# Moving an attention's softmax scaling from VectorE to GpSimd in a one-core hybrid layer

## The chip, the core and the metric

The kernel runs on one core of a Trainium2 chip. A core has a matrix engine (TensorE, PE in the profile; its weight loads are shown as PEld), a vector engine (VectorE, DVE), a scalar engine (ScalarE, ACT), GpSimd (POOL), and a queue engine that issues transfers (SyncE, SP). Each engine takes its instructions in order; engines wait for each other by semaphores. SBUF is the working memory, PSUM the memory that TensorE writes. The metric is the time of one execution in microseconds (us).

## What is computed

One layer of a diffusion backbone over 1024 latent tokens and 256 context tokens, width 1024: a modulated norm, one input projection, a gated delta-rule scan (4 heads of 128, forward and backward), a neighbourhood attention (8 heads of 64), an output projection, and a feed-forward part. The change is in the attention. Each latent query has one softmax over a window of keys and all context keys:

```python
s_win = jnp.einsum("bnqhd,binchd->bhnqic", q_r, k_r).astype(jnp.float32) + bias.astype(jnp.float32)
s_win = jnp.where(col_valid[:, :, None, :], s_win, -jnp.inf)
s_ctx = jnp.einsum("bnqhd,bkhd->bhnqk", q_r, k_ctx).astype(jnp.float32)
s = jnp.concatenate([s_win.reshape(B, H, N_COL_BLK, QB_W, n_win), s_ctx], axis=-1)
p = jax.nn.softmax(s, axis=-1).astype(v.dtype)
...
o = (jnp.einsum("bhnqic,binchd->bnqhd", p_win, v_r)
     + jnp.einsum("bhnqk,bkhd->bnqhd", p[..., n_win:], v_ctx))
```

## The kernel before

The attention is cut into 32 pairs: 4 couples of heads, 2 halves of the grid's rows, 4 blocks of columns. A pair holds two heads u = 0 and 1, each with 128 queries in the partitions and 640 keys (384 of the window, 256 of the context) along a row. So there are 64 heads' tiles in all, and of each small operation below 64.

For one head, `pair` does this. TensorE writes the scores to a PSUM slot `sc` (L100, from `qs`, `kh`, `kl`). VectorE adds the bias tile `bt` to them, writes the sum into `bt` and takes the row maximum into the small tile `mx` (L342, a custom instruction with a second record that reads the maximum out). The maximum is negated (L343), ScalarE takes the exponential of `bt` in place with the row sum (L344), the sum's reciprocal is taken (L345), and `bt` is multiplied by it (L346). In the next step TensorE transposes `bt` in five pieces into another `sc` slot (L104), ScalarE copies them to `pt` (L355), TensorE multiplies with the values (L100, `pt` with `vc` and `vw`), and the result goes to `na` on ScalarE and VectorE (L367, L368).

Buffers tie pairs together. `sc` has three slots, so the transposes of a pair's second head wait for L342 of the next pair's first head, and the next scores for L342 of its second. `bt` has five tiles: before a tile is filled, `biases` clears its context part on GpSimd (L305) and loads the table from `rpb` through SP (L306); both wait until the transposes of five tiles earlier have read it.

The attention runs beside the scan. `fill` is the attention's generator, and the scan's loop takes 0.72 of a step of it after each step of its own. The scan's work on VectorE is L1197, L1208, L1220, L1227 and L1237. In the second half of its ten rounds each chunk is also closed by `finish`: squares (L1252), a reciprocal root on four columns in a chain of tiny operations (L198 to L203), a product (L1258), a transpose of `oacc` (L104) and L1266 to L1268. The last round also starts the output projection: `two_blocks` loads `ew`, and GpSimd takes its low parts (L1292).

What is written in this order is then put in another by a scheduler: it keeps the dependencies and lists each engine's instructions by when it reckons them ready. The order of the engines' instructions is thus a result of the build, and a changed line can move its neighbours.

Of the kernel before, what the change touches and what calls it, by code (L numbers as in the profile page):

```python
# [14 lines left out]
OP = mybir.AluOpType  # L15
# [74 lines left out]
def hybrid(ctx, tc, a, dbg):  # L90
    nc = tc.nc
    act, dve, pool, sp = nc.scalar, nc.vector, nc.gpsimd, nc.sync
# [195 lines left out]
    def attention(nw):  # L288

        def load(hd):  # L290
            qs = nw.tile([128, L], F16, name="qs", tag="qs", bufs=4)
            kh = nw.tile([128, T], F16, name="kh", tag="kh", bufs=4)
            kl = nw.tile([128, T], F16, name="kl", tag="kl", bufs=4)
            sp.dma_start(qs, nq_d[hd].rearrange("i d t -> (i d) t"))
            for i in range(2):
                sp.dma_start(kh[i * 64:i * 64 + 64], nk_d[0, hd])
                sp.dma_start(kl[i * 64:i * 64 + 64], nk_d[1, hd])
            return qs, kh, kl

        def biases(hp, half, cb):  # L300

            out = []
            for u, w0 in enumerate(WIN):
                bt = nw.tile([128, 640], F32, name="bt", tag="bt", bufs=5)
                pool.memset(bt[:, CTX[w0]], 0.0)  # L305
                sp.dma_start(bt[:, w0:w0 + 384], a["rpb"][2 * hp + u, half, CASE[cb]])  # L306
                out.append(bt)
            return out

        def values(hp, half, cb):  # L310
            vw = nw.tile([128, 3, 128], F32, name="vw", tag="vw", bufs=3)
            sp.dma_start(vw, vw_d[:, cb, half:half + 3, hp * 128:hp * 128 + 128])
            return vw

        def context(hp):
            vc = nw.tile([128, 2, 128], F32, name="vc", tag="vc")
            sp.dma_start(vc, nv_d[0:CT, hp * 128:hp * 128 + 128].rearrange("(c p) d -> p c d", p=128))
            return vc

        def slot():  # L320
            return psum[-1].tile([128, 1024], F32, name="sc", tag="sc", bufs=3)

        def pair(heads, bts, vw, vc, half, cb, out):

            r0 = 4 * half
            mx = nw.tile([128, 2, 4], F32, name="mx", tag="mx", bufs=3)
            for u, (head, w0, bt) in enumerate(zip(heads, WIN, bts)):
                qs, kh, kl = head
                sc = slot()[:, AT[u]:AT[u] + 640]
                q = qs[:, (half * 4 + cb) * 128:(half * 4 + cb + 1) * 128]  # L330
                kv = [kx[:, CT:].rearrange("p (r c) -> p r c", c=64)[:, r0:r0 + 12, BLKS[cb]:BLKS[cb] + 32]
                      for kx in (kh, kl)]
                parts = [(CTX[w0].start, CTX[w0].stop, (kh[:, 0:CT], kl[:, 0:CT]))]
                if w0:
                    parts += [(256, 512, [x[:, 0:8] for x in kv]), (512, 640, [x[:, 8:12] for x in kv])]
                else:
                    parts += [(0, 384, kv)]
                for n0, n1, ks in parts:
                    for i in range(2):
                        pe.matmul(sc[:, n0:n1], q, ks[i], start=i == 0, stop=i == 1)  # L340
                m = mx[:, u]
                dve.tensor_tensor_reduce(bt, sc, bt, 1.0, -3.0e38, OP.add, OP.max, m[:, 0:1])  # L342
                dve.tensor_scalar(m[:, 1:2], m[:, 0:1], -1.0, None, op0=OP.mult)  # L343
                act.activation(bt, bt, AF.Exp, bias=m[:, 1:2], accum_out=m[:, 2:3])  # L344
                dve.reciprocal(m[:, 3:4], m[:, 2:3])  # L345
                dve.tensor_scalar(bt, bt, m[:, 3:4], None, op0=OP.mult)  # L346
            yield 1
            pts = []
            for u, bt in enumerate(bts):
                held = slot()  # L350
                sc = held[:, AT[u]:AT[u] + 640]
                for j in range(5):
                    pe.transpose(sc[:, j * 128:(j + 1) * 128], bt[:, j * 128:(j + 1) * 128], ident)
                pt = nw.tile([128, 640], F32, name="pt", tag="pt", bufs=3)
                act.copy(pt, sc)  # L355
                pts.append(pt)
            yield 1
            o = held[:, AT[1] + 640:AT[1] + 768]
            for j in range(5):
                for u, (w0, pt) in enumerate(zip(WIN, pts)):  # L360
                    vals = [vc[:, i] for i in range(2)] + [vw[:, i] for i in range(3)]
                    vv = (vals[j] if w0 else vals[(j + 2) % 5])[:, u * ND:u * ND + ND]
                    pe.matmul(o[u * ND:u * ND + ND], vv, pt[:, j * 128:(j + 1) * 128], start=j == 0, stop=j == 4)
            hi, lo = (out[:, i, half * 512:half * 512 + 512].rearrange("p (r b c) -> p r b c", r=8, b=4)[:, :, cb]
                      for i in range(2))
            o = o.rearrange("p (r c) -> p r c", r=8)
            act.copy(hi, o)  # L367
            dve.tensor_tensor(lo, o, hi.bitcast(F32), OP.subtract)  # L368
            yield 1

        order = [(hp, half, cb) for hp in range(NAH // 2) for half in range(2) for cb in range(4)]
        heads = {0: [load(0), load(1)]}
        vcs = {0: context(0)}
        bt, vw = biases(*order[0]), values(*order[0])
        yield 1
        old = None
        for n, (hp, half, cb) in enumerate(order):
            if half == 1 and cb in (0, 2) and hp + 1 < NAH // 2:
                heads.setdefault(hp + 1, []).append(load(2 * hp + 2 + cb // 2))
                if cb == 0:  # L380
                    vcs[hp + 1] = context(hp + 1)
            cur = pair(heads[hp], bt, vw, vcs[hp], half, cb, na[hp])
            next(cur)
            if old:
                next(old)
            if n + 1 < len(order):
                bt, vw = biases(*order[n + 1]), values(*order[n + 1])
            yield 1
            if old:
                next(old)  # L390
            old = cur
            yield 1
        next(old)
        yield 1
        next(old)
# [967 lines left out]
    class Stream:  # L1363
# [67 lines left out]
        def next(self, n=2):  # L1431

            while len(self.got) < n:
                self.make()
            out = [self.got.pop(0) for _ in range(n)]
            return out
# [400 lines left out]
```

## Time and profile before

| | |
|---|---|
| median of 3 runs | 1521.46 us (1518.48 to 1524.15) |
| the profiled execution | 1521.66 us, span 1519.9 us |
| attention beside the scan | about 553 to 780 us of the span |
| POOL busy in 553 to 680 and 680 to 780 us | 10.99 and 10.56 us |
| granted TensorE clock, mean | 0.99 of full speed |

A row of the stretches shows, for each engine, its busy time. A row of the groups shows line, engine, operation, tiles written and read, shapes and count, then busy us and mean ns of one, then the engine's idle time before it and who ended it. A row of the waits says which engine at which line waited for whom: total us, times, longest. A row of the timeline has start, duration, engine, line and operation, with the idle time before it in brackets. Some matmul records can be missing, and a matmul's record is longer than the time to the next one, since matmuls are pipelined.

### The profile page before, as it was taken

To read this page: it belongs to the slowest core of one execution; us is meant where nothing else is said; L and a number is where in the kernel's file an instruction comes from. 1 tells how busy PE (TensorE), PEld (TensorE's weight loads), DVE (VectorE), ACT (ScalarE), POOL (GpSimd) and SP (SyncE) were. 2 spreads that over 40 slices of the span, in tenths; PEclk is the share of its full clock that TensorE was granted. 3 is DMA by queue.
4 is the path that set the end of the run, shared out by engine and by line. 5 is a ranking of instruction groups with operands and counts; after the bars stand their busy time and mean duration, and the time that the engine had idled before them with its cause. 6 is when DMAs were issued, how large, how long until landed. Compare 5 with 4: busy or idle time off the path is not lost.

```text
span 1519.9 us, 23452 instructions
## 1 busy us (share of the span) xinstructions
PE 1455.5 (96%) x8365; PEld 1208.0 (79%) x8365; DVE 1010.1 (66%) x1908; ACT 703.1 (46%) x1379; POOL 183.3 (12%) x251
## 2 busy tenths in 40 slices
PE   6999998899999998999898999999999999999998
PEld 3789787678877777888787888788888888888887
DVE  4787579455677436779977398766665556699652
ACT  5443461674366545656733284333333334354441
POOL 0154500343134300000100000000000000000000
PEclk9999999999999999999999999999999999999999
DMA  9377133565477798999529415333333335798752
GB/s 368 113 229 238 54 94 122 198 170 176 135 214 251 223 289 239 284 269 274 178 76 322 139 35 183 122 105 103 104 102 101 105 104 172 259 366 284 235 153 83
DMA packets 209829, 276.28 MB, mean 182 GB/s; under 512 B 15968, under 2 KB 116912, under 8 KB 208688
## 3 DMA queue, kind: packets, MB, share of 16 engines
q1 hardware_dynamic: 208992, 274.41, 56.3%
q8 instruction: 66, 1.08, 0.3%
q14 instruction: 51, 0.42, 0.1%
q10 hardware_dynamic: 720, 0.37, 0.1%
HBM read 209.93 MB, written 68.98 MB: 184 GB/s over the span
## 4 chain that ended last, share of the span: by engine, by line
PE 45%; DVE 4%; DMA 2%; ACT 1%; issue 1%; SPq 0%; DVEq 0%; ACTq 0%
PE ps L100 42%; PE sc L100 2%; DMA wad<-wa 1%; PE sc L104 1%; DVE x L1591 1%; DVE ulo L1422 1%; DVE acc L254 0%; DMA wraw<-w_out 0%; DVE x L1567 0%; DVE bt L342 0%; DVE lT L1562 0%; DVE x L1470 0%; ACT x L1571 0%; DVE lB L1575 0%; DMA f_d<-g 0%
## 5 line engine op out<-in xcount | busy, mean ns | idle before, releaser
L100 PE MATMUL ps<-hT,uhi 128*128 128x512 f32 x496 | 146.9, 390 | 1.5 <-DVE e L1712 1.4
L100 PE MATMUL ps<-lT,uhi 128*128 128x512 f32 x496 | 146.5, 390 | 0.0
L100 PE MATMUL ps<-hT,ulo 128*128 128x512 f32 x496 | 146.3, 390 | 0.0
L100 PE MATMUL blk<-hh,whi 128*128 128x512 f32 (+1 forms) x456 | 138.8, 397 | 1.9 <-ACT hh L724 1.5
L100 PE MATMUL blk<-hh,wlo 128*128 128x512 f32 (+1 forms) x456 | 130.0, 378 | 0.0
L100 PE MATMUL ps<-hB,uhi 128*128 128x512 f32 x436 | 129.3, 390 | 0.0
L100 PE MATMUL blk<-hl,whi 128*128 128x512 f32 (+1 forms) x456 | 129.2, 377 | 0.0
L100 PE MATMUL ps<-lB,uhi 128*128 128x512 f32 x436 | 128.9, 390 | 0.0
L100 PE MATMUL ps<-hB,ulo 128*128 128x512 f32 x436 | 128.8, 390 | 0.0
L1421 ACT CAST uhi<-ws 128x512 fp32r<-128x512 f32 x91 | 54.7, 622 | 144.8 <-PE ps L100 81.8
L1421 ACT CAST uhi<-wq 128x512 fp32r<-128x512 f32 x101 | 60.3, 621 | 131.3 <-PE ps L100 70.2
L1422 DVE TENSOR_TENSOR ulo<-wq,uhi 128x512 fp32r<-128x512 f32 x101 | 67.2, 688 | 64.8 <-ACT uhi L1421 35.6
L100 PEld LDWEIGHTS ps<-hT,uhi 128*128 128x128 f32 x496 | 93.0, 188 | 21.3 <-ACT uhi L1421 1.7
L100 PEld LDWEIGHTS ps<-lT,uhi 128*128 128x128 f32 x496 | 93.1, 188 | 19.7 <-DVE lT L1575 0.4
L100 PEld LDWEIGHTS ps<-hT,ulo 128*128 128x128 f32 x496 | 93.2, 188 | 19.3
L100 PEld LDWEIGHTS ps<-hB,uhi 128*128 128x128 f32 x436 | 81.9, 188 | 17.4 <-issue 0.5
L100 PEld LDWEIGHTS ps<-lB,uhi 128*128 128x128 f32 x436 | 81.8, 188 | 17.2 <-DVE lB L1575 0.3
L100 PEld LDWEIGHTS ps<-hB,ulo 128*128 128x128 f32 x436 | 81.9, 188 | 16.9
L100 PEld LDWEIGHTS blk<-hh,wlo 128*128 128x128 f32 x456 | 80.7, 191 | 17.8 <-issue 2.5
L100 PEld LDWEIGHTS blk<-hl,whi 128*128 128x128 f32 x456 | 81.0, 190 | 15.2
L100 PEld LDWEIGHTS blk<-hh,whi 128*128 128x128 f32 x456 | 77.5, 192 | 19.1 <-ACT hh L724 3.2
L1422 DVE TENSOR_TENSOR ulo<-ws,uhi 128x512 fp32r<-128x512 f32 x91 | 60.7, 686 | 36.0 <-ACT uhi L1421 27.9
(337 smaller groups left out, 3051.1 us busy)
## 6 DMA issues: line engine op xcount, KB each, us to landing
wq<-w_fo SPq DMA_DIRECT2D x99, 256.0 KB
wq<-w_gu SPq DMA_DIRECT2D x88, 256.0 KB
wad<-wa SPq DMA_DIRECT2D x64, 256.0 KB
bt<-rpb SPq DMA_DIRECT2D x64, 192.0 KB
t_d<-g SPq DMA_DIRECT2D x22, 512.0 KB
fr<-t_d SPq DMA_DIRECT2D x44, 256.0 KB
f_d<-g SPq DMA_DIRECT2D x33, 256.0 KB
fr<-f_d SPq DMA_DIRECT2D x33, 256.0 KB
```

The lines of the kernel that those rows point to most:

```text
L100: i = nc.tensor.matmul(*args, **kw)
L104: i = nc.tensor.transpose(*args, **kw)
L1421: act.copy(hi, self.raw[key])
L1422: dve.tensor_tensor(lo, self.raw[key], hi.bitcast(F32), OP.subtract)
L1591: dve.tensor_tensor(B[at][:, k], B[x][:, k], B.get(y, B["B11"])[:, k], OP.subtract)
```

## The change

The negation and the product go from VectorE to GpSimd; reciprocals and products are written in a loop of their own, after both heads' exponentials. From here on each line behind the change has a number higher by one: the reciprocal is L346, the product L347.

```diff
                 dve.tensor_tensor_reduce(bt, sc, bt, 1.0, -3.0e38, OP.add, OP.max, m[:, 0:1])
-                dve.tensor_scalar(m[:, 1:2], m[:, 0:1], -1.0, None, op0=OP.mult)
+                pool.tensor_scalar(m[:, 1:2], m[:, 0:1], -1.0, None, op0=OP.mult)
                 act.activation(bt, bt, AF.Exp, bias=m[:, 1:2], accum_out=m[:, 2:3])
-                dve.reciprocal(m[:, 3:4], m[:, 2:3])
-                dve.tensor_scalar(bt, bt, m[:, 3:4], None, op0=OP.mult)
+            for u, bt in enumerate(bts):
+                dve.reciprocal(mx[:, u, 3:4], mx[:, u, 2:3])
+                pool.tensor_scalar(bt, bt, mx[:, u, 3:4], None, op0=OP.mult)
             yield 1
```

On GpSimd, around pair 24 of 0 to 31 (`bt_7269` and `bt_7272` are its tiles and `mx_7337` its maxima; `bt_7158`, `bt_7161` and `mx_7230` are of pair 23, `bt_7376` and `bt_7379` of pair 25, `bt_7443` of pair 26). Before:

```order
L305 MEMSET bt_7269 128x256
L305 MEMSET bt_7272 128x256
L305 MEMSET bt_7376 128x256
L305 MEMSET bt_7379 128x256
L305 MEMSET bt_7443 128x256
```

Now:

```order
L305 MEMSET bt_7376 128x256
L343 TENSOR_SCALAR mx_7230<-mx_7230 128x1
L347 TENSOR_SCALAR bt_7158<-bt_7158,mx_7230 128x640
L343 TENSOR_SCALAR mx_7337<-mx_7337 128x1
L347 TENSOR_SCALAR bt_7161<-bt_7161,mx_7230 128x640
L305 MEMSET bt_7379 128x256
L343 TENSOR_SCALAR mx_7337<-mx_7337 128x1
L347 TENSOR_SCALAR bt_7269<-bt_7269,mx_7337 128x640
L305 MEMSET bt_7443 128x256
```

Negations and products stand between the clearings, and a product can stand behind the next pair's first negation.

On VectorE at the same place, where `finish` closes two chunks (`nwt`, `orr`, `RQ` and `oacc` are its tiles). Before:

```order
L342 ISA bt_7376,mx_7404<-sc_7405,bt_7376 128x640
L342 ISA mx_7404 128x1
L203 SCALAR_TENSOR_TENSOR orr_7280<-nwt_7285,orr_7280 128x4
L201 TENSOR_TENSOR nwt_7321<-orr_7316 128x4
L345 RECIPROCAL mx_7337<-mx_7337 128x1
L201 TENSOR_TENSOR nwt_7285<-orr_7280 128x4
L202 SCALAR_TENSOR_TENSOR nwt_7321<-nwt_7321 128x4
L346 TENSOR_SCALAR bt_7269<-bt_7269,mx_7337 128x640
L202 SCALAR_TENSOR_TENSOR nwt_7285<-nwt_7285 128x4
L203 SCALAR_TENSOR_TENSOR orr_7316<-nwt_7321,orr_7316 128x4
L345 RECIPROCAL mx_7337<-mx_7337 128x1
```

Now:

```order
L342 ISA bt_7272,mx_7337<-sc_7348,bt_7272 128x640
L342 ISA mx_7337 128x1
L201 TENSOR_TENSOR nwt_7285<-orr_7280 128x4
L369 TENSOR_TENSOR na2_4920<-sc_7261,na2_4920 128x8x16
L202 SCALAR_TENSOR_TENSOR nwt_7285<-nwt_7285 128x4
L203 SCALAR_TENSOR_TENSOR orr_7316<-nwt_7321,orr_7316 128x4
L346 RECIPROCAL mx_7337<-mx_7337 128x1
L203 SCALAR_TENSOR_TENSOR orr_7280<-nwt_7285,orr_7280 128x4
L201 TENSOR_TENSOR nwt_7321<-orr_7316 128x4
L1258 TENSOR_TENSOR orr_7280<-orr_7280,RQ_108 128x4
L202 SCALAR_TENSOR_TENSOR nwt_7321<-nwt_7321 128x4
L1259 TENSOR_TENSOR oacc_5092<-oacc_5092,orr_7280 128x512
```

The products and negations are gone, and the root's chain is done before the next pair's reduction (L342 of `bt_7376`), where it used to reach past it.

## The prediction

> **What bounds the kernel now.** I read the page first, for where the change can matter at all, and then the busy times of the stretches around the attention.
>
> ```profile
> PE 1455.5 (96%) x8365; PEld 1208.0 (79%) x8365; DVE 1010.1 (66%) x1908; ACT 703.1 (46%) x1379; POOL 183.3 (12%) x251
> ...
> 553.00:680.00 127.00, 116.17 (x1091) 103.55 (x1090) 89.82 (x297) 78.05 (x210) 10.99 (x33) 0.97 0.93 269
> 680.00:780.00 100.00, 93.06 (x906) 79.45 (x905) 92.33 (x357) 65.73 (x184) 10.56 (x28) 1.00 0.69 197
> 780.00:800.00 20.00, 20.00 (x95) 16.57 (x94) 11.55 (x40) 4.95 (x20) 0.00 (x0) 1.00 0.40 123
> ```
>
> Columns of the last three rows: stretch, its length, then busy time of PE, weight loads, DVE, ACT and POOL, granted clock, DMA share, GB/s. PE is the bound of the whole program. The attention and the scan share 553 to 780 us, and there PE is idle for 127.00 - 116.17 = 10.8 us early and 100.00 - 93.06 = 6.9 us late: 17.8 us in all, the most that any relief can win. DVE differs between the two parts: 71% busy early, 92% late. So DVE is a second bound only in the last 100 us. What PE waits for in each part (engine, line, who ended the wait: total us, times, longest), late first, then early:
>
> ```profile
> PE sc L100 <- ACT pt L355: 3.0, 5, 1.1
> PE sc L100 <- DVE mx L342: 1.5, 2, 1.0
> PE sc L104 <- DVE mx L342: 1.4, 4, 0.5
> PE sc L104 <- DVE na L368: 0.3, 1, 0.3
> PE ps L100 <- DVE vn L1197: 0.3, 1, 0.3
> ...
> PE sc L104 <- DVE mx L342: 6.8, 4, 2.1
> PE sc L104 <- DVE bt L346: 2.0, 1, 2.0
> PE sc L100 <- ACT pt L355: 0.8, 2, 0.7
> ...
> DVE bt L342 <- DMA bt<-rpb: 11.6, 5, 4.1
> ```
>
> L342 is the reduction that adds the bias to the scores; when it ends, a score slot in PSUM comes free for the next transposes or scores. Late, PE waits 3.5 us for DVE and 3.0 us for ACT's copy of the transposed tile (L355), which itself follows the transposes. Early, the 6.8 us are mostly another matter: the last row says that L342 then waited 11.6 us in 5 places for the bias table to land, which no engine's relief hastens.
>
> Why L342 and its successors are late in the second part is seen in one stretch of the DVE's timeline, with ACT's next exponential behind it:
>
> ```profile
> 727.12 0.08 DVE L342 DVE_READ_ACCUMULATOR2_ANT mx<- 128x1 f32 x1
> ...
> 727.47 0.55 DVE L346 TENSOR_SCALAR bt<-bt,mx 128x640 f32<-128x640 f32 x1
> ...
> 728.29 0.55 DVE L346 TENSOR_SCALAR bt<-bt,mx 128x640 f32<-128x640 f32 x1
> ...
> 728.90 0.14 DVE L343 TENSOR_SCALAR mx<-mx 128x1 f32<-128x1 f32 x1
> ...
> 729.13 0.83 ACT L344 ACTIVATE bt<-bt,mx 128x640 f32<-128x640 f32 x1 [1.44 <-issue]
> ```
>
> The maximum is there at 727.20, but its negation starts at 728.90, behind two products (L346) and a dozen tiny operations, most of the root that closes the scan's rows; the exponential starts at 729.13 after ACT sat idle 1.44 us. This is a queue, not work.
>
> A microsecond won here is won at the end. PE runs without a gap to the close of the stage, and only then does the next stage's weight load go out:
>
> ```profile
> 789.23 2.79 PE sc L100 x12
> ...
> 792.95 0.03 SPq L217
> 792.98 0.03 issue
> 793.01 6.96 DMA wraw<-w_out
> ```
>
> **The change part by part.** First what DVE loses: 64 products and 64 negations.
>
> ```profile
> L342 DVE CUSTOM_DVE_ANT_0 bt<-sc,bt 128x640 f32<-128x640 f32 x64 | 51.8, 819 | 46.5 <-issue 32.2 <-DMA bt<-rpb 11.6 <-PE sc L104 2.0
> L346 DVE TENSOR_SCALAR bt<-bt,mx 128x640 f32<-128x640 f32 x64 | 35.1, 549 | 0.5
> ...
> L346 DVE TENSOR_SCALAR bt<-bt,mx 128x640 f32<-128x640 f32 x30 | 16.4, 548 | 0.0
> ...
> L343 DVE TENSOR_SCALAR mx<-mx 128x1 f32<-128x1 f32 x30 | 4.7, 156 | 0.0
> ```
>
> The last two rows are of 680 to 780 us alone: 16.4 + 4.7 = 21.1 us of 92.3 at most (records overlap their neighbours a little), so DVE falls from 92% to 71-75% there, the level of the early part. The queue in front of L342 and of the exponentials then mostly goes. Of the 6.5 us that PE waits late I take 5 as won: the 3.5 for DVE, and half of the 3.0 for ACT's copies, whose transposes stood behind late products. Early, of the waits not due to the table, 2.0 + 0.8 us, I take 1. Bounds: 0 and 17.8 us.
>
> Next what POOL gets. It shows no such product; these are its nearest rows:
>
> ```profile
> L680 POOL CAST mr<-masks x1: 609/609/609, 43.8 to 43.8; 128x512 fp32r<-128x512 f32 x1
> ...
> L597 POOL COPY WK<-kk x16: 442/452/908, 95.0 to 153.6; 32x320 f32<-32x320 f32 x16
> ...
> L220 POOL TENSOR_TENSOR wlo<-wraw,whi x21: 2377/2407/3166, 75.2 to 529.1; 128x1024 fp32r<-128x1024 f32 x21
> ...
> L679 POOL COPY wide<-sc x1: 198/198/198, 4.8 to 4.8; 128x16 f32<-128x16 f32 x1
> ```
>
> By the cast, 640 elements take 609 x 640/512 = 0.76 us; by the copy, 2 x 0.452 = 0.90; by the two-input subtraction, 2.407 x 640/1024 = 1.50. The product reads one tile and one value per partition, so it is nearest to the first two: I take 0.85 us, with 0.76 and 1.50 as ends. 64 x 0.85 = 54 us over a stage of 227 us in which POOL was busy for 21.6: it fits. The negation is like the 16-element copy, 0.2 us. The Trainium skill ("GPSIMD Engine Reference", section Engine selection) says that work with one input runs there at roughly line rate and work with two about twice as slow as on VectorE; by line rate, 640 elements at the page's 1.2 GHz would be an estimated 0.53 us, no longer than on DVE, and the sum would be 0.5 us better. The cast's row, nearly 1.2 ns an element, is short of that rate.
>
> A product is thus 0.3 us longer, and with one more hand-over between engines (0.09 us from L343's end at 729.04 to the exponential) 0.4 us later. It costs only where the transposes start as soon as it ends. In the trace 12 of the 64 start within 0.5 us of their product's end, the first and one of the last being:
>
> ```profile
> 558.89 0.55 DVE L346 TENSOR_SCALAR bt<-bt,mx 128x640 f32<-128x640 f32 x1
> 559.59 0.63 PE L104 MATMUL sc<-cst,bt 128*128 128x128 f32 x4 [1.95 <-DVE bt L346]
> ...
> 767.85 0.55 DVE L346 TENSOR_SCALAR bt<-bt,mx 128x640 f32<-128x640 f32 x1
> 768.50 0.63 PE L104 MATMUL sc<-cst,bt 128*128 128x128 f32 x4
> ```
>
> 12 x 0.4 = 4.8 us if nothing came earlier. But the negation leaves a queue that cost 1.7 us in the place above, so most products start earlier than now: I charge 0.5 us, with 0 and 4.8 as ends.
>
> POOL's queue is in order, and the clearing of the next tiles (L305) waits for transposes:
>
> ```profile
> POOL bt L305 <- PE sc L104: 94.8, 31, 11.5
> ```
>
> Until now nothing stood behind those waits. Now negations and products do: in the new order most negations have a clearing ahead of them whose tile is freed by transposes about two pairs older. Set against the times of before, those transposes end after the negation's own start in 10 of 64 places, all but one by under 0.8 us (worked out from L343's and L104's starts one by one). The worst:
>
> ```profile
> 646.08 0.14 DVE L343 TENSOR_SCALAR mx<-mx 128x1 f32<-128x1 f32 x1
> ...
> 647.17 0.71 PE L104 MATMUL sc<-cst,bt 128*128 128x128 f32 x5
> ```
>
> There the negation would wait from 646.08 past 647.88, with the exponential and all that ACT has behind it. I charge 0.5 us and leave 3 as the upper end. The reciprocals stay on DVE and wait for the exponentials as before. That both exponentials are written ahead of both products alters little: they are neighbours on ACT already. The bias-table loads wait on SP for the same transposes as now, and DMA is no tighter.
>
> One more price is contention, shown before the attention: POOL's two-input subtraction, and DVE's 256-element product beside it and alone.
>
> ```profile
> 410.83 2.39 POOL L220 TENSOR_TENSOR wlo<-wraw,whi 128x1024 fp32r<-128x1024 f32 x1 [15.33 <-ACT whi L218]
> ...
> 411.06 2.32 DVE L491 TENSOR_SCALAR cacc<-cr,cw 128x256 f32<-128x256 f32 x1 [4.87 <-ACT cr L482]
> ...
> 462.73 0.35 DVE L491 TENSOR_SCALAR cacc<-cr,cw 128x256 f32<-128x256 f32 x1 [1.11 <-ACT cr L482]
> ```
>
> DVE's 0.35 us became 2.32, to the very end of POOL's instruction. So some DVE work can lose up to a product's 0.85 us. I charge 0.5 us of PE time, with 0 and 6 as ends (30 late products x half of 0.85 = 12.7 us of DVE time if each caught such work, half of it felt).
>
> Sum: -5.0 - 1.0 + 0.5 + 0.5 + 0.5 = -4.5 us, against the profiled execution's own 1521.66 us (span 1519.9), which stands 0.2 above the median of the runs shown: 1517 us.
>
> **The rivals.** *The whole queue goes.* All of the late 6.9 us and the early waits not due to the table (10.8 less some 7 us) are won, about 10 us, at no cost: 1511 us. For it: PE has no other bound late, and the exponential's wait is queueing. Against it: one-off waits move rather than vanish, and the scheduler has put PE's work in another order.
>
> *Nothing is gained.* PE is at its rate and the waits pass to POOL's products: 1521 us. For it: 93 of 100 us busy.
>
> *Slower, by POOL's product.* At 1.50 us each, with the second of a pair queued behind the first, the second ends some 1.5 to 2 us later than now. In the trace 24 of the 64 transposes start less than 2 us after their product; at about 0.8 us mean loss that is 19 us, less the 6 won: 1535 us. It decides from a product of about 1.1 us on, where loss passes gain. Against it: the cast and copy rows.
>
> *The lock.* DVE instructions that read two SBUF tiles (the scan's root and its product with the outputs) stand still beside POOL's products and give the relief back: the 6 us of the upper end make 1517 + 6 = 1523 us. It leans on the 2.32 us row. The Trainium skill ("SBUF — State Buffer", section Who interferes with whom) speaks against the change here: a DVE instruction with two SBUF inputs, or in a two-port mode, and a GpSimd one that reads SBUF exclude each other for their whole length. The 2.32 us agree for the two-port case; for two inputs beside a product no row here shows it.
>
> **How the numbers follow.** A measurement of this kernel can tell about 0.5%, 7.6 us. Chances: the forecast (1514 to 1520) 0.38, the whole queue 0.28, nothing gained 0.09, the lock 0.10, slower by POOL's product 0.15. Faster by over 0.5% (below 1514) is the second and the lower edge of the first: 0.35. Slower by over 0.5% (above 1529) is the last with a little of the lock: 0.18. Within: 0.47. The range reaches from 1508 (the second with some early waits too) to 1527 (the lock and a product of over 1 us), leaving out about 2 in 10.
>
> **What would show it.** Right: POOL rows of 64 products at 0.76 to 0.90 us; DVE at most 78 busy of 100 us late; exponentials starting within 0.6 us of the maximum; PE's waits for L342 late under 1.5 us; the stage's close 4 to 5 us earlier. Wrong: products above 1.1 us, PE or weight loads waiting for POOL by several us, tiny DVE operations of 0.5 us and more beside products, or a clearing that holds a negation back.

## The result, and the profile after

The changed kernel took 1534.18 us (median of 6 runs, 1531.82 to 1538.71) against 1523.03 us of the kernel before (6 runs): a ratio of 1.008, with a 95% interval of 1.006 to 1.0099. The forecast was 1517 us, the range 1508 to 1527. It is slower, by 11 us. The profiled execution has a span of 1530.0 us, 10.1 more than before.

The stretches of the changed kernel (columns as in the prediction: PE, weight loads, DVE, ACT, POOL):

```profile
553.00:680.00 127.00, 114.40 (x1061) 101.60 (x1059) 69.68 (x228) 76.70 (x207) 80.84 (x101) 0.96 0.91 263
680.00:780.00 100.00, 84.12 (x810) 72.19 (x809) 79.70 (x276) 63.56 (x180) 70.22 (x87) 0.98 0.66 197
```

VectorE is relieved as meant: in the late part it falls from 92.33 to 79.70 us of 100. But TensorE's idle time grows from 17.8 us to 12.6 + 15.9 = 28.5 us, and GpSimd, which was nearly idle, is busy for 64% and 70% of the two parts. Its groups from 540 to 800 us say by what:

```profile
L347 POOL TENSOR_SCALAR bt<-bt,mx 128x640 f32<-128x640 f32 x64 | 121.8, 1906 | 15.7 <-DVE mx L346 13.5 <-issue 1.1 <-DMA qT<-qT_d 0.8
L305 POOL MEMSET bt<- 128x256 f32 x59 | 18.3, 313 | 25.3 <-PE sc L104 25.2
L343 POOL TENSOR_SCALAR mx<-mx 128x1 f32<-128x1 f32 x64 | 15.3, 240 | 57.2 <-DVE mx L342 51.7 <-DVE mx L346 2.8 <-DMA qT<-qT_d 1.8
```

The product takes 1.906 us on GpSimd; on VectorE it took 0.549. The negation takes 0.24 us, as was reckoned. What TensorE waits for from 553 to 800 us:

```profile
PE sc L104 <- POOL bt L347: 9.9, 8, 3.7
PE sc L100 <- ACT pt L356: 6.1, 11, 1.0
PE sc L104 <- POOL bt L305: 4.4, 3, 1.6
PE sc L104 <- DVE na L369: 3.9, 2, 1.9
PE sc L104 <- DMA bt<-rpb: 1.9, 1, 1.9
```

The waits for L342 (9.7 us before) and the product's 2.0 on VectorE are gone. In their place are 9.9 us for GpSimd's products, 4.4 for its clearings, and 3.9 for L369 (0.3 before, as L368). Two other in-order engines stand longer as well, ScalarE at the exponential and VectorE at the reciprocal that follows it; before, then now, from 553 to 800 us:

```profile
ACT bt L344 <- DVE mx L343: 11.7, 7, 4.3
DVE mx L345 <- ACT bt L344: 10.8, 13, 1.7
...
ACT bt L344 <- POOL mx L343: 42.9, 32, 3.7
DVE mx L346 <- ACT bt L344: 30.3, 26, 6.1
```

Where the waits for L369 come from is seen in one stretch of the timeline, which comes back at each of the last three pairs of chunks that `finish` closes; DVE, POOL, ACT and PE in turn:

```profile
734.84 0.08 DVE L342 DVE_READ_ACCUMULATOR2_ANT mx<- 128x1 f32 x1
...
737.94 0.16 DVE L346 RECIPROCAL mx<-mx 128x1 f32<-128x1 f32 x1 [1.75 <-ACT bt L344]
738.03 0.75 DVE L1267 SCALAR_TENSOR_TENSOR z<-ps,onw,z 128x512 f32<-128x512 f32 x1
738.69 0.28 DVE L369 TENSOR_TENSOR na<-sc,na 128x128 fp32r<-128x128 f32 x1
...
734.55 0.31 POOL L305 MEMSET bt<- 128x256 f32 x1
734.84 1.91 POOL L347 TENSOR_SCALAR bt<-bt,mx 128x640 f32<-128x640 f32 x1
736.72 0.23 POOL L343 TENSOR_SCALAR mx<-mx 128x1 f32<-128x1 f32 x1
...
736.98 0.83 ACT L344 ACTIVATE bt<-bt,mx 128x640 f32<-128x640 f32 x1 [3.10 <-POOL mx L343]
737.72 0.18 ACT L344 ACTIVATION_READ_ACCUMULATOR bt<-bt,mx 128x1 f32 x1
737.81 0.24 ACT L368 CAST na<-sc 128x128 fp32r<-128x128 f32 x1
...
739.23 0.74 PE L104 MATMUL sc<-cst,bt 128*128 128x128 f32 x5 [1.94 <-DMA bt<-rpb]
```

The maximum is there at 734.92. Its negation stands on GpSimd behind the previous pair's product and starts at 736.72. ScalarE stands at the exponential for 3.10 us, 2 of them after the maximum was there, and has the cast L368 behind it, whose sources had been ready for about 2 us. VectorE stands 1.75 us at the reciprocal, which needs the same exponential, and has L1267 and L369 behind it. L369 needs the cast too and starts at 738.69; only then is the score slot free, and the transposes start at 739.23, 2 us late. The row's own label names a table transfer; the wait that ended last in the other two such places is L369. So one product costs through three queues, GpSimd's, then ScalarE's and VectorE's. The stage closes late by 10.8 us, all of the loss in the span:

```profile
800.02 2.79 PE sc L100 x12
803.80 6.83 DMA wraw<-w_out
```

### The profile page after: what moved, and what is told of

Same layout as the page of the kernel before. It is cut to its first block, busy times and chain, and to the rows that moved or that the text cites. A ratio compares the mean times of both kernels' runs of the same rounds, so it can differ in the third digit from the quotient of the medians.

```text
span 1530.0 us, 23444 instructions
## 1 busy us (share of the span) xinstructions
PE 1455.7 (95%) x8365; PEld 1208.1 (79%) x8365; DVE 984.7 (64%) x1780; ACT 704.4 (46%) x1379; POOL 317.7 (21%) x379
## 4 chain that ended last, share of the span: by engine, by line
PE 68%; DVE 11%; DMA 9%; ACT 5%; issue 4%; POOL 3%; SPq 1%; ACTq 0%; DVEq 0%; POOLq 0%
PE ps L100 44%; PE blk L100 14%; PE sc L100 3%; PE pr L100 3%; PE m L100 2%; POOL bt L347 2%; DMA nv_d<-zt 2%; DMA wad<-wa 2%; DVE cacc L477 1%; PE sc L104 1%; DVE acc L254 1%; DMA wraw<-w_nqk 1%; DMA xt<-xcT 1%; DVE bt L342 1%; ACT bt L344 1%
## 5 line engine op out<-in xcount | busy, mean ns | idle before, releaser
L347 POOL TENSOR_SCALAR bt<-bt,mx 128x640 f32<-128x640 f32 x64 | 121.8, 1906 | 15.7 <-DVE mx L346 13.5
L100 PEld LDWEIGHTS blk<-hh,wlo 128*128 128x128 f32 x456 | 80.4, 190 | 17.8 <-issue 1.7
```

The source lines that it names most:

```text
L100: i = nc.tensor.matmul(*args, **kw)
L347: pool.tensor_scalar(bt, bt, mx[:, u, 3:4], None, op0=OP.mult)
```

## Experiments: which part costs

Each kernel was timed in turn with the kernel before on the same chip, whose median in the five groups of runs was 1522.24, 1521.69, 1522.16, 1522.74 and 1522.49 us. The theories at first: A, the product's own 1.9 us, for which TensorE waits; B, GpSimd's in-order queue, where negations stand behind clearings; C, the order that the scheduler makes of the changed lines.

*The negation alone* (before, with one line changed):

```diff
-                dve.tensor_scalar(m[:, 1:2], m[:, 0:1], -1.0, None, op0=OP.mult)
+                pool.tensor_scalar(m[:, 1:2], m[:, 0:1], -1.0, None, op0=OP.mult)
```

> The kernel before with the negation alone on GpSimd; product and written order as before. Theory A (the product's 1.91 us on GpSimd, against 0.55 on VectorE, is what costs): no loss, 1518 to 1523 us, since VectorE loses 9 us of small work and the exponentials leave its queue; POOL shows 64 negations of about 0.23 us. Theory B (GpSimd's order in one queue holds negations behind clearings that wait for transposes, and exponentials with them): 1526 us or more. Theory C (the written order and what the scheduler makes of it): about 1523.

Measured: 1523.32 us, ratio 1.0011 (0.9993 to 1.003). Clearings ahead of a negation cost 0.3% at most by themselves: B in this form falls.

*The product alone* (before, with one line changed):

```diff
-                dve.tensor_scalar(bt, bt, m[:, 3:4], None, op0=OP.mult)
+                pool.tensor_scalar(bt, bt, m[:, 3:4], None, op0=OP.mult)
```

> The kernel before with the product alone on GpSimd; negation on VectorE, written order as before. Theory A: most of the loss, 1530 to 1537 us, with products of 1.9 us and TensorE waiting for them by about 10 us. Theory B: little loss, 1522 to 1526, since no negation stands behind a product or a clearing. Theory C: about 1523.

Measured: 1525.33 us, ratio 1.0027 (1.0013 to 1.0041). TensorE waits for the product more than in the changed kernel, and yet the loss is 3 us:

```profile
PE sc L104 <- POOL bt L346: 14.3, 15, 3.3
```

*The written order alone* (the changed kernel, both operations on `dve`):

> The changed kernel's written order (both exponentials ahead of both reciprocals and products), but negation and product on VectorE. Theories A and B: as before within 2 us, 1521 to 1525. Theory C: a good part of the loss, 1528 to 1534.

Measured: 1521.08 us, ratio 1.0001 (0.9986 to 1.0017). C falls.

The parts cost 1, 3 and 0 us, together 11. *The product in the new order*, the negation on VectorE, looks for a pairing of these two:

```diff
-                pool.tensor_scalar(m[:, 1:2], m[:, 0:1], -1.0, None, op0=OP.mult)
+                dve.tensor_scalar(m[:, 1:2], m[:, 0:1], -1.0, None, op0=OP.mult)
```

> The changed kernel with the negation back on VectorE: product on GpSimd, written order of the change. Against 1522.2 us of before: the queue theory (the 8 us that neither edit costs alone come from negations that stand behind 1.9 us products in GpSimd's one queue) gives what the product costs alone, 1524 to 1527. The order theory (the new order is harmful only once the product is slow) gives 1531 to 1535, as the whole change.

Measured: 1525.45 us, ratio 1.0018 (1.0 to 1.0036). The order does not matter with a slow product either. *Both on GpSimd in the order of before* is the pairing that is left (before, with the first two edits):

> Negation and product both on GpSimd, but in the written order of before, so that the second head's negation always stands behind the first head's product, which waits for that head's exponential. Queue theory: the second exponential starts 1.9 us of product later than it could, the pair's second product ends 1 to 2 us later than in the changed kernel, and the time is above the changed kernel's: 1537 to 1555 us. If only the product's own 1.9 us count, or the new order is what hurts: 1525 to 1534 us.

Measured: 1537.75 us, ratio 1.0113 (1.0091 to 1.0136), at the low end of the queue theory's range. The new order is thus a little better than the old one, and the loss comes when negation and product share GpSimd's queue.

*Does anybody need the product for that?* The real product goes back to VectorE, and GpSimd multiplies a scratch tile of 128x320 twice in its place, with negations on GpSimd (first kernel) or on VectorE (second):

```diff
-                pool.tensor_scalar(bt, bt, mx[:, u, 3:4], None, op0=OP.mult)
+                dve.tensor_scalar(bt, bt, mx[:, u, 3:4], None, op0=OP.mult)
+                for _ in range(2):
+                    pool.tensor_scalar(idle, idle, mx[:, u, 3:4], None, op0=OP.mult)
```

> The changed kernel with the real product on VectorE; GpSimd runs, in the product's place in its queue, two multiplications of 128x320 on a scratch tile that nobody reads (about 1.9 us together), and the negations. Nobody waits for the multiplications but what stands behind them in the queue and the release of the small tile. Queue theory: negations are late as in the changed kernel, part of the 8 us shows: 1526 to 1531. Theory of the product's own length (TensorE waits for its output): 1522 to 1524, as with the negation alone. Theory of contention (VectorE's instructions stretched beside GpSimd's): the same loss here as in the run without negations on GpSimd.

> The same scratch multiplications on GpSimd, negation and product both on VectorE: nothing of the attention waits for GpSimd but the clearings. Contention theory: VectorE's two-input instructions stretch, 1524 to 1529 us. Queue theory and theory of the product's own length: 1521 to 1523 us, the clearings being late at most.

Measured: 1544.41 us, ratio 1.0157 (1.0133 to 1.0181), with the negations on GpSimd; 1525.5 us, ratio 1.0033 (1.0015 to 1.0052), with them on VectorE. Nobody reads the scratch tile; the same multiplications cost 4 us, and 19 us more as soon as negations stand behind them. This is more than the queue theory expected, partly since the two pieces are 1.206 us each, 2.4 us for 1.9. Contention does not explain the 19 us: VectorE's product takes 615 ns with the negations on GpSimd and 638 with them on VectorE (549 before). The waits of TensorE and ScalarE, first with negations on GpSimd:

```profile
PE sc L100 <- ACT pt L358: 21.8, 21, 2.1
...
ACT bt L344 <- POOL mx L343: 42.0, 29, 3.8
```

and with them on VectorE:

```profile
PE sc L100 <- ACT pt L358: 3.0, 6, 1.2
...
ACT bt L344 <- DVE mx L343: 10.7, 6, 4.2
```

ScalarE stands at exponentials for 42.0 us, and TensorE for 21.8 us at the copies (`pt`) that ScalarE has behind them. One such place in the first kernel:

```profile
696.64 2.27 POOL L349 TENSOR_SCALAR idle<-idle,mx 128x320 f32<-128x320 f32 x2
698.85 0.32 POOL L305 MEMSET bt<- 128x256 f32 x1
699.13 0.46 POOL L343 TENSOR_SCALAR mx<-mx 128x1 f32<-128x1 f32 x1
...
699.62 0.83 ACT L344 ACTIVATE bt<-bt,mx 128x640 f32<-128x640 f32 x1 [1.25 <-POOL mx L343]
700.36 0.19 ACT L344 ACTIVATION_READ_ACCUMULATOR bt<-bt,mx 128x1 f32 x1
700.45 0.67 ACT L358 COPY pt<-sc 128x640 f32<-128x640 f32 x1
...
701.18 0.32 PE L100 MATMUL sc<-pt,vc 128*64 128x128 f32 x1 [1.50 <-ACT pt L358]
```

The maximum was there at 697.54, its negation came at 699.13 behind two scratch multiplications and a clearing; the copy behind the exponential, whose transposes had ended at 698.36, started at 700.45, and TensorE stood 1.50 us. (The built orders of these two kernels differ a little as well; the negation alone, at 1 us, and the order alone, at 0, speak against that as the cause, but no run has the one order with the other placement.)

## Experiments: how the loss goes with the piece's length

*The product in the two-input form* (the changed kernel):

```diff
-                pool.tensor_scalar(bt, bt, mx[:, u, 3:4], None, op0=OP.mult)
+                pool.tensor_tensor(bt, bt, mx[:, u, 3:4].to_broadcast([128, 640]), OP.mult)
```

> The changed kernel with GpSimd's product written as a two-tile product (the tile times its reciprocal, broadcast along the row). Theory A: the time follows the product's length. By the two-input rows of before (2.407 us for 1024 elements) it takes 1.50 us in place of 1.91, 30% of the way back to VectorE's 0.55, so about 1531 us. If the length is not what counts, 1534 as the changed kernel; if the form is slower still, above 1534.

Measured: 1527.55 us, ratio 1.0041 (1.0024 to 1.0059), and the product is shorter in this form:

```profile
L347 POOL TENSOR_TENSOR bt<-bt,mx 128x640 f32<-128x640 f32 x64 | 80.0, 1254 | 19.0 <-DVE mx L346 14.3 <-PE sc L104 1.2 <-DMA bt<-rpb 1.2
```

*The product halved*, each engine taking half of the columns:

```diff
-                pool.tensor_scalar(bt, bt, mx[:, u, 3:4], None, op0=OP.mult)
+                pool.tensor_scalar(bt[:, 0:320], bt[:, 0:320], mx[:, u, 3:4], None, op0=OP.mult)
+                dve.tensor_scalar(bt[:, 320:640], bt[:, 320:640], mx[:, u, 3:4], None, op0=OP.mult)
```

> The changed kernel with each product split: columns 0 to 319 on GpSimd, 320 to 639 on VectorE beside it. GpSimd's piece is about 1.2 us (the length of a 128x320 product in the run with scratch multiplications), VectorE's about 0.3. Queue and length theory: as with the two-input form of 1.254 us, 1526 to 1529 us, less what VectorE's earlier half does not help. If the loss grew with the number of GpSimd's instructions and not with their length: 1534 us as the whole change.

Measured: 1516.09 us, ratio 0.9964 (0.9945 to 0.9982), below both theories, and faster than both kernels. GpSimd's piece, VectorE's piece and the stretches:

```profile
L347 POOL TENSOR_SCALAR bt<-bt,mx 128x320 f32<-128x320 f32 x64 | 76.2, 1194 | 13.9 <-DVE mx L346 9.8 <-DMA qT<-qT_d 1.4 <-issue 0.9
...
L348 DVE TENSOR_SCALAR bt<-bt,mx 128x320 f32<-128x320 f32 x64 | 29.4, 462 | 0.5
...
553.00:680.00 127.00, 119.67 (x1127) 105.49 (x1125) 88.46 (x274) 80.63 (x218) 59.44 (x106) 0.99 0.95 278
680.00:780.00 100.00, 90.78 (x882) 78.35 (x881) 87.60 (x322) 64.76 (x190) 50.30 (x83) 1.00 0.65 186
```

TensorE's idle time is 7.3 + 9.2 = 16.5 us, 12 us less than in the changed kernel. VectorE's half takes 462 ns, not 0.3 us, so VectorE is relieved of only 5.7 us of products (35.1 before) and stays at 87.60 us late. No negation starts more than 0.91 us after its maximum; in the changed kernel 11 of 64 start more than 1 us after it, the latest 2.29 us (L343's start less the end of L342's second record, one by one). Lateness alone is not the loss: before, 26 of 64 start more than 1 us after it, the latest 4.12, but ScalarE stood at exponentials for 17.5 us only, and for 43.8 in the changed kernel. Nor is the sum of these stands: the half left out (below) has 32.1 us of them, the longest 2.8, and loses nothing.

*256 columns on GpSimd, 384 on VectorE* (the same edit, with 256 for 320):

> The halved product with 256 columns on GpSimd and 384 on VectorE. From 1.194 us at 320 columns and 1.906 at 640, 256 columns are estimated at about 1.05 us. If the time follows GpSimd's length: 1 to 3 us faster, 1513 to 1515 us. If VectorE's share is the limit now: 1517 to 1519 us.

Measured: 1519.64 us, ratio 0.9987 (0.9966 to 1.0009). The piece took 1.064 us, as estimated, but the time did not follow it further down.

*The halved product with the negation on VectorE*:

> The halved product with the negation on VectorE; GpSimd holds clearings and the 1.2 us pieces. If negations on GpSimd still lose by the queue: 1512 to 1515 us. If the relief by the negation's 64 instructions is worth more than the queue costs: 1517 to 1520 us. Same within a microsecond or two of 1516: neither counts any more.

Measured: 1521.74 us, ratio 0.9997 (0.9976 to 1.0018). In this pair of builds, with a 1.2 us piece, the negation on GpSimd gains rather than loses.

*Half of the product left out*: GpSimd scales columns 0 to 319 and nobody the rest, in the form of the change (first) and in the two-input form (second), so that only length and form differ:

> The changed kernel with the product on columns 0 to 319 alone, on GpSimd; the other half stays unscaled, so part of the work is left out. GpSimd's piece is that of the halved product without VectorE's piece beside it, estimated at 1.1 us from the shortest ones there. If the halved product is limited by GpSimd's piece: the same as the halved product, 1514 to 1518 us. If its VectorE piece still costs: 1509 to 1513 us.

> The same columns, with the product in the two-input form, estimated at 0.65 us from 1.254 us at 640 columns: half the length in the queue, the same columns left out. If only length in the queue counts: 1 to 4 us faster than the run before it. If the two-input form hurts beside its length (in the changed kernel with it VectorE's 128x4 instructions took 337 ns in place of 199): the same or slower, by up to 5 us.

Measured: 1520.05 us, ratio 0.9992 (0.9978 to 1.0006), and 1520.76 us, ratio 0.999 (0.9979 to 1.0002), with pieces of 1.102 and 0.721 us:

```profile
L347 POOL TENSOR_SCALAR bt<-bt,mx 128x320 f32<-128x320 f32 x64 | 70.4, 1102 | 18.6 <-DVE mx L346 16.6 <-issue 1.1 <-DMA qT<-qT_d 0.8
```

```profile
L347 POOL TENSOR_TENSOR bt<-bt,mx 128x320 f32<-128x320 f32 x64 | 46.1, 721 | 25.2 <-DVE mx L346 21.0 <-DMA y<-y_d 1.8 <-issue 1.0
```

Shorter pieces and less work on VectorE than in the halved kernel, and no gain over it. In the form of the change the loss goes between 1.9 and 1.2 us, in the two-input form between 1.25 and 0.72; below that no run shows a gain from a shorter piece, and what remains is a scatter of a few us between builds. The last column is from one execution each: the time from the start of the first L342 to the start of the last result that goes to `na` on VectorE.

| kernel, negations on GpSimd | GpSimd's piece, us | against before, us | attention, us |
|---|---|---|---|
| before (negations on VectorE) | none | 0 | 224.9 |
| negation alone | none | +1.1 | 221.6 |
| half left out, two-input | 0.721 | -1.7 | 224.9 |
| 256 columns | 1.064 | -3.1 | 224.5 |
| half left out | 1.102 | -2.4 | 222.1 |
| halved | 1.194 | -6.1 | 222.0 |
| two-input | 1.254 | +5.3 | 228.7 |
| changed kernel | 1.906 | +11.2 | 237.0 |
| scratch multiplications | 2 x 1.206 | +22.7 | 247.5 |

The halved kernel's attention is thus no shorter than that of the half left out, though its time is 4 us less. What does differ is the granted clock: 0.9913 in the mean of its seven executions, 0.9893 in the eleven of the half left out. Over the 124 executions of the kernel before under 1530 us the mean is 0.9889, and a straight line through them gives an estimated 1.6 us less time for each 0.001 of clock. By that line some 3 of the 4 us, and over half of the 6 us against before, go with the clock; whether the kernel or chance made the clock higher was not tested.

## Experiments: clearings, and relief without GpSimd

*The clearings on VectorE* in the changed kernel:

```diff
-                pool.memset(bt[:, CTX[w0]], 0.0)
+                dve.memset(bt[:, CTX[w0]], 0.0)
```

> The changed kernel with the clearings of 128x256 on VectorE, so that GpSimd's queue holds negations and products only. If clearings are what holds negations back, or what is held back with the biases' transfers behind them: 5 us or more come back, 1525 to 1529 us. If the products hold the negations back: 1531 to 1536 us, since the products stay, and VectorE has 59 more instructions.

Measured: 1527.59 us, ratio 1.0035 (1.0019 to 1.005): 6 us come back. So the clearings are a part of the changed kernel's loss after all, though not of the negation's alone: between products they add to the queue, and TensorE's 4.4 us for L305 go. In the profiled executions the attention is 2.7 us shorter than the changed kernel's, so a part of the 6 lies elsewhere. Whether by their own 0.3 us or by standing until a tile is released was to be told by *six bias tiles* in place of five:

```diff
-                bt = nw.tile([128, 640], F32, name="bt", tag="bt", bufs=5)
+                bt = nw.tile([128, 640], F32, name="bt", tag="bt", bufs=6)
-            vw = nw.tile([128, 3, 128], F32, name="vw", tag="vw", bufs=3)
+            vw = nw.tile([128, 3, 128], F32, name="vw", tag="vw", bufs=2)
```

> The changed kernel with 6 bias tiles in place of 5 (and 2 value tiles in place of 3, for room), so that a clearing in GpSimd's queue finds its tile free earlier; nothing leaves the queue. If the queue stands at clearings whose tile TensorE has not yet released, and negations and products stand behind: 3 to 7 us come back, 1527 to 1531 us, and GpSimd's idle time before clearings (25.2 us in the changed kernel) falls to under 10. If it is the clearings' own 0.3 us, or only the products' length: 1533 to 1536 us.

Measured: 1531.54 us, ratio 1.0058 (1.0034 to 1.0082). It is inconclusive: GpSimd's idle time before clearings only fell from 25.2 to 22.2 us, so the edit did not take away what it was to take away. *The halved product with the clearings on VectorE*:

> The halved product with the clearings on VectorE. If clearings in the queue still hold negations and products back with a piece of 1.2 us: 2 to 5 us faster than the halved product alone, 1511 to 1514 us. If with the short piece the queue has room, it is the same or, for 59 more instructions of about 0.27 us on VectorE, slower: 1516 to 1520 us.

Measured: 1536.47 us, ratio 1.0093 (1.0057 to 1.013), outside both expectations: 20 us above the halved product. Now VectorE's queue stands at clearings, 8.5 us in 5 places, and TensorE waits again for what VectorE has behind them:

```profile
PE sc L100 <- ACT pt L357: 8.3, 15, 1.1
PE sc L104 <- POOL bt L347: 6.7, 3, 3.0
PE sc L100 <- DVE mx L342: 4.8, 2, 3.8
PE sc L104 <- DVE mx L342: 2.3, 1, 2.3
...
DVE bt L305 <- PE sc L104: 8.5, 5, 4.2
```

In the halved kernel the waits for L342 are 0.6 us and those for the product 3.0. Of the 20 us 17 lie in the attention (239.1 us for 222.0). That the stand at clearings is the cause was not shown: in the changed kernel with its clearings on VectorE that stand is 11.4 us, and 6 us came back. The granted clock was lower too, 0.97 in both parts for 0.99 and 1.00.

*VectorE relieved without GpSimd*: the reciprocal scales the identity, and TensorE multiplies each block by that diagonal in place of the transpose:

```diff
-                dve.tensor_scalar(bt, bt, m[:, 3:4], None, op0=OP.mult)
+                dve.tensor_scalar(dg, ident, m[:, 3:4], None, op0=OP.mult)
...
-                    pe.transpose(sc[:, j * 128:(j + 1) * 128], bt[:, j * 128:(j + 1) * 128], ident)
+                    pe.matmul(sc[:, j * 128:(j + 1) * 128], bt[:, j * 128:(j + 1) * 128], dgs[u], start=True, stop=True)
```

> Before, with the product taken off the 640 columns: VectorE scales the 128x128 identity by the reciprocal sum, and TensorE multiplies each block by that diagonal in place of the transpose (both forms last 278 ns in the trace of before), both exponentials ahead of both. VectorE is relieved without GpSimd. If VectorE's relief is worth what the prediction gave it once nobody waits for a slow product: 5 to 10 us faster than before, 1512 to 1518 us. If TensorE's own work and ScalarE set the pace and the relief is worth nothing: 1520 to 1523 us.

> The same with the negation on GpSimd, whose queue now holds clearings and negations only. Queue theory: nothing long stands ahead of a negation, so this is within 2 us of the same kernel with the negation on VectorE. If the negation's place on GpSimd costs by itself (its 240 ns and two more semaphores per head): 3 us or more above it.

Measured: 1540.09 us, ratio 1.0116 (1.0092 to 1.014), and 1542.3 us, ratio 1.0128 (1.0106 to 1.0151). The first misses both expectations, since it made work for TensorE:

```profile
L100 PE MATMUL sc<-dg,bt 128*128 128x128 f32 x640 | 78.2, 276 | 1.9 <-DVE dg L349 1.7 <-issue 0.2
```

Before, the transposes were 320 records with 46.1 us. Each f32 block now is two, and TensorE, the bound, is busy for 32 us more. As a test of the relief it failed. The pair still answers the second question: with no long piece in GpSimd's queue the negation there costs 2.2 us, not 19. It is a weak test, since TensorE is busy for 97 of 100 us late in both.

## Why the prediction was wrong, point by point

*The product's price* is the step that failed first. It was taken at 0.85 us with 0.76 and 1.50 as ends, scaled from a cast, a copy and a two-input subtraction, because those were the rows that GpSimd had. It measured 1.906, above all three. The product by a value per partition is not "nearest to the first two": it was slower than the form with two inputs (1.254 us). The sentence on the Trainium skill ("GPSIMD Engine Reference", section Engine selection), by which one-input work runs near line rate, gave an estimated 0.53 us; the measurement decides against it here.

*POOL's in-order queue*, taken at 0.5 us with 3 as the end, is the second, and the larger in time. The prediction asked only what clearings hold back. It did not ask what a product holds back, though the order that it showed has a product ahead of a negation; and it did not go on to ScalarE, where copies and casts stand behind the exponential that waits, or back to VectorE, whose reciprocals were to wait for exponentials "as before" and stood 30.3 us for 10.8. In the changed kernel 6 to 7 of the 11 us are what neither move costs alone. The scratch multiplications show that this path costs 19 us when the piece is 2.4 us long, though nobody waits for its output.

*VectorE's relief* was right as a mechanism (VectorE at 79.70 us late, where 78 at most was forecast; the waits for L342 gone) and taken too large, at 6 us. With the negation gone and the product gone or short, the runs give 1.7 to 3.1 us, with intervals that reach to nothing, and one build 6.1, over half of it with a higher clock; from the half left out, the intervals leave at most 3.4 us (0.9978). Some of what was won at L342 shows up again at ScalarE's copies: 6.1 us in the changed kernel for 3.8 before.

*The rival "slower by POOL's product"* gave 1535 us, and 1534.18 came. That the numbers meet is partly luck: it reckoned with products of 1.50 us and with transposes that wait for them. Its turning point of about 1.1 us was not far off: 1.194 us still won and 1.254 lost, though in kernels that differ in form too. Its mechanism was half of it: transposes that wait for products are 9.9 us of TensorE's new waits, but with the negation on VectorE a product of the same length costs only 3 to 4 us.

*The lock* was taken at 0.5 us. VectorE's product of the outputs, which reads two tiles (684 ns before), and one of the root's small steps (L202, 154 ns) did stretch, from 680 to 780 us:

```profile
L1259 DVE TENSOR_TENSOR oacc<-oacc,orr 128x512 f32<-128x512 f32 x6 | 7.0, 1161 | 0.1
L202 DVE SCALAR_TENSOR_TENSOR nwt<-nwt 128x4 f32<-128x4 f32 x18 | 4.6, 255 | 0.0
```

L201 and L203, the root's other repeated steps, kept 154 and 153 ns; of the 18 L202, three took about 0.7 us. The row of L1259 agrees with the rule cited from the Trainium skill ("SBUF — State Buffer", section Who interferes with whom) for two SBUF inputs, for which no row stood before. These two are some 5 us of VectorE's time late. In time the part of L1259 is roughly bounded by the product in the new order, with the negation on VectorE: L1259 takes 984 ns there (L202 stays at 154), and that whole kernel costs 3.8 us.

```profile
L1259 DVE TENSOR_TENSOR oacc<-oacc,orr 128x512 f32<-128x512 f32 x6 | 5.9, 984 | 0.0
```

*Exponentials within 0.6 us of the maximum*: 25 of 64 in the changed kernel for 5 before, median 0.79 us for 1.69 (L344's start less L342's end, one by one). The gain that the forecast rested on did take place in most places, and exponentials more than 2 us after their maximum fell as well, from 20 to 11. What was lost is not seen in this measure; it is seen in single long stands of ScalarE and VectorE with ready work behind them, as in the place shown above (3.10 and 1.75 us).

Open is which way the clearings cost, and what gave the halved kernel its clock. Differences of 3 to 5 us between neighbouring builds, with another order of all engines each, were not explained by length.

## What to carry to other kernels

Before moving an operation to an engine, find a row of that very operation and operand form on it; where there is none, let the forecast hang on the price as an unknown, since a row of a similar operation was off by more than two here. Then ask of the new queue what a long instruction holds back, and follow it through the next in-order engine: a short operation that others wait for should not share a queue with a long one that nobody hurries for. A split that kept the longest piece short (here 1.2 us) took the queue's loss away; that it also wins was not shown apart from the clock.

## What was not expected of the hardware

On GpSimd, the multiplication by a value per partition took 1.906 us for 128x640 f32 and 1.102 us for 128x320, 2.5 ns for each further element of a row; the same product with that value broadcast as a second input took 1.254 and 0.721 us, 1.7 ns an element. VectorE's product of 128x640 rose from 549 to 638 ns beside scratch multiplications on GpSimd. And a f32 matmul with a 128x128 diagonal shows twice the records of the transpose of the same block.
